# Attention of a two-layer trunk: heads handled in pairs, probabilities times v as 512-column products

## The chip, the cores and the metric

One core of a Trainium2 chip runs the whole kernel as one program. The metric is the device time of one execution in microseconds (us), the median of several runs. The engines are TensorE (PE in the profile, with its weight loads as PEld), VectorE (DVE), ScalarE (ACT), GpSimd (POOL) and SyncE (SP, which issues most DMAs).

## The reference

Two layers are computed on a latent stream (256 tokens) and a context stream (256 tokens), each 2048 wide. Each layer projects the normalized, modulated input into three branches; the one that matters here is attention: 8 query heads of 128, 2 key/value heads (4 query heads share one), rotary positions on the latent tokens, a learned sink in the softmax. Latent queries see 256 context keys and their window of latent keys in one softmax; context queries see context keys only. Context is needed from layer 0 alone, so layer 1 has latent queries only.

```python
s_loc = where(mask, q @ kw * scale, NEG_INF);  s_ctx = q @ k_ctx * scale
p = softmax(concat([sink, s_ctx, s_loc]))
o = p_ctx @ v_ctx + p_loc @ vw                 # latent queries, 256 x 128 per head
p = softmax(concat([sink, q_c @ k_c * scale])) # context queries, layer 0
o_c = p[..., 1:] @ v_c
y = concat([gMLP * silu(g), attention * silu(g), fourier * silu(g)]) @ w_out
```

Everything is float32 in and out.

## The kernel before

**Precision and products.** The kernel computes float32 products from pairs: every operand is split into a high part (`fp32r`, rounded by a copy on ACT, line 507) and a low part (the rest, by a subtraction on DVE, line 508: `split_into`). A product is then three: hi x hi, hi x lo, lo x hi (`mm3`, lines 489 to 492). In layer 1 the latent input holds both halves side by side, so that a step is one product of 512 columns (line 627) and one of 256 (line 629); ACT copies one half of the sum and DVE adds the other (`joined`, lines 609 to 614).

**Units.** The input projection is a chain of units of PE work, one for 128 output columns: `tunit` (layer 0, both streams, 512 columns) and `tunit1` (layer 1). Weights come through the stream `W`: a DMA into a raw tile, a high half on ACT (whi, line 458), a low half on DVE (wlo, line 460). In between, `pace` feeds steps of the modulation, which DVE computes alone (`mod_dve`, lines 250 and 252, and `mod_gate1`, line 290).

**Order.** PE's order is the order of the program text as it is run. Work that needs results of other engines is put off by generators: `later.add(attention(h, ps))` starts one for each head after its q unit, each `yield x` lets x us of units pass (planned time, counted by `later.tick`), and `later.flush` ends all. `YQ`, `YA` and `YB` (line 344) are the pauses of attention in the two layers: from q to scores, from scores to transposes, and between transposes. The order of ACT, DVE and the DMA queues is set by a scheduler from the same program.

**Attention** (lines 944 to 1013), per head: rotate q (`rope`, four copies on ACT, three operations on DVE, then the split into a hi and a lo tile); scores into `ps_sc` (and `ps_scc` for context queries in layer 0); mask and maximum on DVE; exponentials on ACT into probability tiles, two of 128x512 and in layer 0 a third for the context queries; scale by 1/den on ACT (line 985). Then in halves (three in layer 0, two in layer 1): four transposes of 128x128 into `ps_tp` (line 1005), split into a hi and a lo tile of 512 columns, and, one step later, six products of 256 columns with v into `ps_o` (`pv`, by `mm3`). A half is two key blocks of 128 x two query blocks. At the end one copy of o on ACT (line 1013). Gate units (`bg`) follow the eight q units, and multiply o by silu of the gate; `flush` runs before the last of them.

**Rooms.** Temporaries of 128x512 (2 KB per partition) come from one pool of seven tiles, `w2k` (lines 74 and 81): the probabilities, q's halves, the halves of split transposes, and the temporary of `rope`. PSUM has six tiles `mm` (units, scores, o) and two `ms` (transposes). `rots` are four rooms of 128x256 in a tile `mgl`, used by `rope` in turn (line 929). Tiles `yo4` to `yo11` receive the heads' outputs in layer 0 and are empty until then; `hl0` to `hl7` are empty in layer 1 after the projection's context part; `acc`, `rbs` and `join` have other uses earlier or later.

Of the kernel before, what the change touches and what calls it, by code (L numbers as in the profile page):

```python
# [7 lines left out]
F32 = mybir.dt.float32  # L8
F32R = mybir.dt.float32r
BF16 = mybir.dt.bfloat16  # L10
AF = mybir.ActivationFunctionType
ALU = mybir.AluOpType

P = 128
D = 2048
KT = D // P
S = 256
T = 2 * S
EPS = 1e-6
SCALE = 128 ** -0.5  # L20
# [46 lines left out]
def trunk_kernel(ctx: ExitStack, tc: tile.TileContext, xT, xhalf, cT, wss, wsl, wmod, win, wout0, wout1, const, vec, rows,  # L67
                 wmat, bs, sink, out):
    nc = tc.nc
    V, A, G, PE, DMA = nc.vector, nc.scalar, nc.gpsimd, nc.tensor, nc.sync  # L70
# [6 lines left out]
    def sb(shape, dt, tag, bufs=1):  # L77
        cnt[0] += 1
        return pool.tile(shape, dt, tag=tag, bufs=bufs, name=f"{tag}_{cnt[0]}")

    def w2k(shape, dt=F32):
        return sb(shape, dt, "w2k", W2K)

    def mm_ps(name="mm"):
        cnt[0] += 1
        return psum.tile([P, 512], F32, tag="mm", bufs=6, name=f"ps_{name}_{cnt[0]}")

    def ms_ps(name="ms"):
        cnt[0] += 1
        return psum.tile([P, 512], F32, tag="ms", bufs=2, name=f"ps_{name}_{cnt[0]}")  # L90


    yo = [sb([P, T], F32, f"yo{k}") for k in range(KT)]
# [42 lines left out]
    ident = identr.bitcast(F32)  # L136
# [204 lines left out]
    YH = 2.0  # L341
    NX, AHEADX, LATE = 4, 2, 12
    YX, YC, YE = [2.4, 1.4, 1.8], 1.5, 5.0
    YQ, YA, YB = [5.5, 6.8], [10.0, 8.6], [3.8, 4.0]

    def pace():

# [141 lines left out]
    def mm3(ps, st, mv, start, stop):  # L489
        PE.matmul(ps, st[0], mv[0], start=start, stop=False)  # L490
        PE.matmul(ps, st[0], mv[1], start=False, stop=False)  # L491
        PE.matmul(ps, st[1], mv[0], start=False, stop=stop)  # L492

    def part(w, c):

        def of(t):
            if not isinstance(t, list):
                return t[:, c]
            n = t[0].shape[-1]
            return t[c.start // n][:, c.start % n:c.start % n + c.stop - c.start]  # L500

        return of(w[0]), of(w[1])
# [3 lines left out]
    def split_into(hi, lo, src):  # L506
        A.copy(hi, src)  # L507
        V.tensor_tensor(out=lo, in0=src, in1=hi.bitcast(F32), op=ALU.subtract)  # L508
        return hi, lo
# [36 lines left out]
    hl = [None] * KT  # L546
# [42 lines left out]
    FULL, LAT, CTX = slice(0, T), slice(0, S), slice(S, T)  # L589
# [54 lines left out]
    def layer(l):  # L644
        last = l == 1
        n = S if last else T
        nt = n // P
        ysl = (lambda k: y1[k] if k < 4 else yo[k][:, S:T]) if last else (lambda k: yo[k])
        y1 = {}
        if last:  # L650
            a = sb([P, 4, 256], F32, "macc")
            c = [sb([P, 2, S], F32, f"kt{j}") for j in range(2)]
# [166 lines left out]
        if l == 0:  # L819
# [4 lines left out]
            with low(LOWC):  # L824
                for name in ("m0", "ct", "nst"):
                    o, w = COFF[name]
# [97 lines left out]
        def rope(hi, lo, ps, ctx=None):  # L924

            if ctx is None and hi.shape[-1] > S:
                ctx = ps[:, S:T]
            nrot[0] += 1
            rot = rots[nrot[0] % 4]
            for a in range(4):  # L930
                b = a ^ 1
                A.copy(rot[32 * a:32 * a + 32], ps[32 * b:32 * b + 32, 0:S])
            t = w2k([P, S])
            V.tensor_tensor(out=t, in0=ps[:, 0:S], in1=cc("cos"), op=ALU.mult)
            V.tensor_tensor(out=rot, in0=rot, in1=cc("sin"), op=ALU.mult)
            V.tensor_tensor(out=rot, in0=rot, in1=t, op=ALU.add)
            split_into(hi[:, LAT], lo[:, LAT], rot)
            if hi.shape[-1] > S:
                split_into(hi[:, CTX], lo[:, CTX], ctx)

        kt, vv = [], None
        rots, nrot = [], [0]

        def attention(h, ps):
            g = h // 4
            q = w2k([P, n], F32R), w2k([P, n], F32R)
            rope(*q, ps)
            yield YQ[l]
            sc, mx = [], sb([P, 4], F32, "mx", 2)
            for b in range(2):  # L950
                s = mm_ps("sc")
                mm3(s, part(q, slice(b * P, (b + 1) * P)), kt[g], True, True)
                edge = s[:, (1 - b) * P:(2 - b) * P]
                V.tensor_tensor(out=edge, in0=edge, in1=split["m0"][:, b], op=ALU.add)
                sc.append((s, T))
                V.tensor_reduce(out=mx[:, b:b + 1], in_=s, axis=mybir.AxisListType.X, op=ALU.max)
            if not last:
                s = mm_ps("scc")
                for b in range(2):
                    mm3(s[:, b * S:(b + 1) * S], part(q, slice(S + b * P, S + (b + 1) * P)),  # L960
                        part(kt[g], CTX), True, True)
                sc.append((s, S))
                V.tensor_reduce(out=mx[:, 2:4], in_=s.rearrange("p (b k) -> p b k", k=S),
                                axis=mybir.AxisListType.X, op=ALU.max)
            nm = sb([P, 4], F32, "nm", 2)
            V.tensor_scalar(out=nm[:, :nt], in0=mx[:, :nt], scalar1=-SCALE, scalar2=nskb[:, h:h + 1],
                            op0=ALU.mult, op1=ALU.min)
            es = sb([P, 4], F32, "es", 2)
            A.activation(es[:, :nt], nm[:, :nt], AF.Exp, bias=skb[:, h:h + 1])
            den = sb([P, 4], F32, "den", 2)  # L970
            prob = []
            for i, (s, w) in enumerate(sc):
                p = w2k([P, T])
                for b in range(T // w):
                    c = i + b
                    A.activation(p[:, b * w:(b + 1) * w], s[:, b * w:(b + 1) * w], AF.Exp, scale=SCALE,
                                 bias=nm[:, c:c + 1], accum_out=den[:, c:c + 1])
                prob.append(p)
            V.tensor_tensor(out=den[:, :nt], in0=den[:, :nt], in1=es[:, :nt], op=ALU.add)
            V.reciprocal(den[:, :nt], den[:, :nt])  # L980
            for i, (s, w) in enumerate(sc):
                for b in range(T // w):
                    c = i + b
                    with low(LOWP[l]):
                        A.activation(prob[i][:, b * w:(b + 1) * w], prob[i][:, b * w:(b + 1) * w], AF.Copy,  # L985
                                     scale=den[:, c:c + 1])
            yield YA[l]
            o, pts = None, []

            def pv(half):  # L990
                for j in range(2):
                    kk = 2 * half + j
                    dst, kv = (o[:, LAT], kk) if half < 2 else (o[:, CTX], 2 + j)
                    mm3(dst, part(vv, slice(kv * 256 + g * P, kv * 256 + (g + 1) * P)),
                        part(pts[half], slice(j * S, (j + 1) * S)), kk in (0, 4), kk in (3, 5))

            halves = 2 if last else 3
            for half in range(halves):
                tp = ms_ps("tp")
                for j in range(2):  # L1000
                    for b in range(2):
                        kk = 2 * half + j
                        src = prob[b][:, kk * P:(kk + 1) * P] if half < 2 else \
                            prob[2][:, b * S + j * P:b * S + (j + 1) * P]
                        PE.transpose(tp[:, (2 * j + b) * P:(2 * j + b + 1) * P], src, ident)  # L1005
                pts.append(split_into(w2k([P, 512], F32R), w2k([P, 512], F32R), tp))
                if half == 0:
                    o = mm_ps("o")
                else:
                    pv(half - 1)  # L1010
                yield YB[l]
            pv(halves - 1)
            A.copy(ysl(4 + h), o[:, 0:n])

        def gate(k, ps):
            assert not last or k < 4 or k in state["ctx"]
# [29 lines left out]
            later.flush()  # L1046
        r = sb([P, 4, S], F32, "mgl")
        state["phase"] = f"k{l}"
        rots += [r[:, i] for i in range(4)]
        for j in range(2):  # L1050
            pss = tunit1([0, 1]) if last else [tunit(T)]
            kt.append((sb([P, T], F32R, f"kt{j}"), sb([P, T], F32R, ("ws", "bsb")[j])))
# [2 lines left out]
        vv = sb([P, 1024], F32R, "vv"), sb([P, 1024], F32R, "mg")  # L1055
        vps = [mm_ps("v") for _ in range(4)]
        for k in range(KT):
            if k % 4 == 0:
                w = W.next()
# [9 lines left out]
        for h in range(8):  # L1069
            ps = tunit1([0])[0] if last else tunit(n)  # L1070
            later.add(attention(h, ps))
            later.tick(0.0)
# [8 lines left out]
        src = [ysl(k) for k in range(KT)]  # L1081
# [153 lines left out]
    rbs = {}  # L1235
# [90 lines left out]
    with tc.manual_schedule(engines={EN.PE}):  # L1326
# [11 lines left out]
        for k in range(KT):  # L1338
# [7 lines left out]
            c = slice(32 * (k % 4), 32 * (k % 4) + 32)  # L1346
# [28 lines left out]
        make_h(0, 0, rb0, [0, 1], e)  # L1375
        list(e)
        layer(0)
        state["acc"] = out_proj()
        layer(1)
        finish()  # L1380

# [76 lines left out]
```

## Time and profile before

| | before |
|---|---|
| runs (median, lowest to highest) | 1128.75 us (1128.7 to 1129.28), n = 3 |
| the profiled execution: time / span | 1129.38 us / 1127.6 us |
| mean granted clock of PE | 0.999 |
| PE busy, share of span | 1118.0 us, 99% |
| DVE busy | 927.4 us, 82% |
| ACT busy | 526.8 us, 47% |
| DMA, mean | 209 GB/s |

The span is the time from the first to the last instruction of the trace; the profiled execution's time holds 1.8 us more around it. A row of a timeline has start (us), time taken (us), engine, line, operation, output<-input by the program's names, and shape; in square brackets stands the idle time before it and who ended it. Products on PE are pipelined: a row's time is longer than the distance to the next start, and the distance is what PE pays.

### The profile page before, as it was taken

Reading aid. Unit: us, or ns where it says so; the run is one execution under the profiler, and the core shown is the slowest. Engines: PE = TensorE matmul, PEld = TensorE weight load, DVE = VectorE, ACT = ScalarE, POOL = GpSimd, SP = SyncE. Lnnn points to the kernel's source line nnn. Section 1 sums busy time; section 2 is a strip of 40 time slices with the busy share of each in tenths; the row PEclk is TensorE's granted clock in tenths of the full one; section 3 lists DMA queues with packets and bytes.
Section 4 is the critical chain, followed back from the end, with each engine's and each line's share of the span. In section 5 each row is a group of like instructions: output and inputs, shape, how many; then the busy total and the mean of one; then the engine's idle time right before and its main releaser. Section 6 shows DMA issues by size and latency. Waiting matters only on the chain.

```text
span 1127.6 us, 16631 instructions
## 1 busy us (share of the span) xinstructions
PE 1118.0 (99%) x6105; PEld 920.2 (82%) x6108; DVE 927.4 (82%) x1633; ACT 526.8 (47%) x992; POOL 32.8 (3%) x43
## 2 busy tenths in 40 slices
PE   8999999999999999999999999999999999999998
PEld 3666788888888888888888888988888888888886
DVE  1578799989988897888999988396898689968883
ACT  5322433322234667632523334266665369867551
POOL 0000000000000000000000000030500000000000
PEclk9999999999999999999999999999999999999999
DMA  9999656566655343365556665285956786555972
GB/s 360 402 402 400 245 175 202 172 204 193 217 183 187 116 142 130 122 205 172 184 181 215 219 208 185 94 191 200 223 172 199 223 286 206 160 163 187 301 263 75
DMA packets 75138, 235.85 MB, mean 209 GB/s; under 512 B 8608, under 2 KB 13104, under 8 KB 75056
## 3 DMA queue, kind: packets, MB, share of 16 engines
q1 hardware_dynamic: 70272, 229.79, 60.7%
q0 software_dynamic: 4064, 3.69, 2.2%
q10 hardware_dynamic: 720, 1.31, 0.3%
q8 instruction: 48, 0.79, 0.3%
q14 instruction: 34, 0.28, 0.1%
HBM read 232.65 MB, written 2.10 MB: 208 GB/s over the span
## 4 chain that ended last, share of the span: by engine, by line
PE 97%; DVE 1%; DMA 1%; ACT 0%; issue 0%; POOLq 0%; DVEq 0%; POOL 0%; ACTq 0%
PE ps_t L490 15%; PE ps_t L491 15%; PE ps_t L492 15%; PE ps_t L627 10%; PE ps_t L629 5%; PE ps_v L1063 3%; PE ps_y L490 3%; PE ps_y L492 3%; PE ps_y L491 3%; PE ps_mod L182 2%; PE ps_av L490 2%; PE ps_av L491 2%; PE ps_av L492 2%; PE ps_tp L1005 2%; PE ps_v L1065 1%; PE ps_au L490 1%
## 5 line engine op out<-in xcount | busy, mean ns | idle before, releaser
L458 ACT CAST whi<-raw 128x1024 fp32r<-128x1024 f32 (+1 forms) x209 | 216.4, 1037 | 314.1 <-PE ps_t L491 219.4
L460 DVE TENSOR_TENSOR wlo<-raw,whi 128x1024 fp32r<-128x1024 f32 (+1 forms) x209 | 251.0, 1205 | 57.3 <-ACT whi L458 47.1
L490 PE MATMUL ps_t<-hh,whi 128*128 128x512 f32 (+1 forms) x752 | 290.7, 387 | 0.0
L491 PE MATMUL ps_t<-hl,whi 128*128 128x512 f32 (+1 forms) x752 | 289.6, 385 | 0.0
L492 PE MATMUL ps_t<-hh,wlo 128*128 128x512 f32 (+1 forms) x752 | 289.4, 385 | 0.0
L252 DVE SCALAR_TENSOR_TENSOR macc<-mraw,cs,macc 128x512 f32<-128x512 f32 x360 | 251.0, 748 | 11.1 <-DMA mraw<-in_wmod_dram 10.9
L492 PEld LDWEIGHTS ps_t<-hh,wlo 128*128 128x128 f32 x752 | 141.3, 188 | 28.6
L490 PEld LDWEIGHTS ps_t<-hh,whi 128*128 128x128 f32 x752 | 141.3, 188 | 27.0
L491 PEld LDWEIGHTS ps_t<-hl,whi 128*128 128x128 f32 x752 | 141.4, 188 | 26.1
L627 PE MATMUL ps_t<-hh,whi 128*128 128x512 f32 x512 | 139.2, 395 | 0.0
L627 PEld LDWEIGHTS ps_t<-hh,whi 128*128 128x128 f32 x512 | 91.4, 189 | 15.0
L629 PEld LDWEIGHTS ps_t<-hh,wlo 128*128 128x128 f32 x512 | 71.5, 190 | 4.5
L629 PE MATMUL ps_t<-hh,wlo 128*128 128x256 f32 x512 | 74.9, 282 | 0.0
L572 ACT ACTIVATE hh<-w2k,sh 128x256 fp32r<-128x256 f32 x48 | 22.0, 502 | 73.6 <-DVE w2k L568 73.6
L490 PE MATMUL ps_y<-whi,hh 128*128 128x512 f32 x104 | 41.3, 398 | 0.0
L492 PE MATMUL ps_y<-whi,hh 128*128 128x512 f32 x104 | 40.6, 390 | 0.0
L491 PE MATMUL ps_y<-wlo,hh 128*128 128x512 f32 x104 | 40.5, 389 | 0.0
L490 PE MATMUL ps_av<-whi,hh 128*128 128x512 f32 x94 | 39.0, 415 | 0.6 <-ACT hh L572 0.6
L491 PE MATMUL ps_av<-wlo,hh 128*128 128x512 f32 x94 | 37.0, 394 | 0.0
L507 ACT CAST w2k<-ps_tp 128x512 fp32r<-128x512 f32 x40 | 23.3, 582 | 21.1 <-PE ps_scc L491 13.7
L508 DVE TENSOR_TENSOR w2k<-ps_tp,w2k 128x512 fp32r<-128x512 f32 x40 | 27.5, 687 | 3.3 <-ACT w2k L507 2.0
L985 ACT ACTIVATE w2k<-w2k,den 128x512 f32<-128x512 f32 (+1 forms) x48 | 28.1, 645 | 0.4 <-DVE den L980 0.2
(460 smaller groups left out, 1721.9 us busy)
## 6 DMA issues: line engine op xcount, KB each, us to landing
raw<-in_win_dram SPq DMA_DIRECT2D x160, 512.0 KB, 4.1
mraw<-in_wmod_dram SPq DMA_DIRECT2D x128, 512.0 KB, 4.3
raw<-in_wout_dram SPq DMA_DIRECT2D x60, 512.0 KB, 4.3
mraw<-in_wsl_dram SPq DMA_DIRECT2D x14, 512.0 KB, 7.2
yo<-in_wsl_dram SPq DMA_DIRECT2D x16, 256.0 KB, 7.1
macc<-in_wsl_dram SPq DMA_DIRECT2D x7, 512.0 KB, 7.8
vv<-in_wsl_dram SPq DMA_DIRECT2D x7, 512.0 KB, 8.4
mg<-in_wsl_dram SPq DMA_DIRECT2D x7, 512.0 KB, 9.0
```

The costliest lines, as they stand in the source:

```text
L252: V.scalar_tensor_tensor(out=acc[:, s], in0=w[:, kk % 2], scalar=c, in1=acc[:, s], op0=ALU.mult, op1=ALU.add)
L458: A.copy(ph, rc)
L460: self.last = V.tensor_tensor(out=pl, in0=rc, in1=ph.bitcast(F32), op=ALU.subtract)
L490: PE.matmul(ps, st[0], mv[0], start=start, stop=False)
L491: PE.matmul(ps, st[0], mv[1], start=False, stop=False)
L492: PE.matmul(ps, st[1], mv[0], start=False, stop=stop)
L507: A.copy(hi, src)
L508: V.tensor_tensor(out=lo, in0=src, in1=hi.bitcast(F32), op=ALU.subtract)
L627: PE.matmul(ps, wk, h, start=k == 0, stop=False)
L629: PE.matmul(ps[:, 0:S], wk, h[:, 0:S], start=False, stop=k == KT - 1)
L985: A.activation(prob[i][:, b * w:(b + 1) * w], prob[i][:, b * w:(b + 1) * w], AF.Copy, scale=den[:, c:c + 1])
L1063: PE.matmul(vps[t], hs[t][0], wk, start=k == 0, stop=False)
```

## The change

Heads are taken in pairs (0 and 1, 2 and 3, ...). The even head ends after its softmax and parks its probabilities; after the odd head's softmax a new generator, `pair_pv`, does transposes and products of both: each step kk takes one key block of 128 for both heads (two heads x two query blocks = four transposes), splits the 512 columns, and one step later multiplies them with v in three products of 512 columns, low half first. Layer 0 has six steps a pair (four for latent, two for context queries), layer 1 four. o of a pair is one PSUM tile of 512 columns for latent queries and one for context queries; ACT copies it in two pieces of 256.

Rooms (`room`): in layer 1 all probabilities lie in `hl0` to `hl7`, two per head, the first four heads' rooms being used again by the last four. In layer 0 an odd head keeps three `w2k` tiles; heads 0 and 2 lie in `yo4` to `yo9`, heads 4 and 6 in `yo10`, `acc`, two `rbs`, and `yo11`, the upper half of `mgl` and two `join`. For that `rope` uses two rooms of `mgl` in layer 0 instead of four. `YB` of layer 0 goes from 3.8 to 3.4.

```diff
-    YQ, YA, YB = [5.5, 6.8], [10.0, 8.6], [3.8, 4.0]
+    YQ, YA, YB = [5.5, 6.8], [10.0, 8.6], [3.4, 4.0]
...
+        paired = {}
+        def room(h):
+            def thirds(t):
+                return [t[:, 0:S], t[:, S:T]]
+            if last:
+                return [sb([P, T], F32, f"hl{h % 4 * 2 + i}") for i in range(2)]
+            if h % 2:
+                ts = [w2k([P, T]) for _ in range(3)]
+            elif h < 4:
+                ts = yo[4 + 3 * h // 2:7 + 3 * h // 2]
+            else:
+                ts = [yo[8 + h // 2], sb([P, T], F32, "acc") if h == 4 else spare]
+                return ts + [[sb([P, S], F32, "rbs" if h == 4 else "join", 2) for _ in range(2)]]
+            return ts[:2] + [thirds(ts[2])]
+
+        def pair_pv(g, h):
+            o, pts = {}, []
+            def pv(kk):
+                kv, dst = (kk, o[0]) if kk < 4 else (kk - 2, o[1])
+                st, (hi, lo) = part(vv, slice(kv * 256 + g * P, kv * 256 + (g + 1) * P)), pts[kk]
+                for a, b in ((st[0], lo), (st[0], hi), (st[1], hi)):
+                    PE.matmul(dst, a, b, start=kk in (0, 4) and b is lo, stop=kk in (3, 5) and a is st[1])
+                if kk in (3, 5):
+                    for i in range(2):
+                        A.copy(ysl(4 + h - 1 + i)[:, slice(kk // 5 * S, kk // 5 * S + S)], dst[:, i * S:(i + 1) * S])
+            for kk in range(4 if last else 6):
+                tp = ms_ps("tp")
+                for i in range(2):
+                    for b in range(2):
+                        pr = paired[h - 1 + i]
+                        src = pr[b][:, kk * P:(kk + 1) * P] if kk < 4 else pr[2][b][:, (kk - 4) * P:(kk - 3) * P]
+                        PE.transpose(tp[:, (2 * i + b) * P:(2 * i + b + 1) * P], src, ident)
+                pts.append(split_into(w2k([P, 512], F32R), w2k([P, 512], F32R), tp))
+                if kk % 4 == 0:
+                    o[kk // 4] = mm_ps("o")
+                if kk:
+                    pv(kk - 1)
+                yield YB[l]
+            pv(len(pts) - 1)
...
-            prob = []
+            paired[h] = prob = room(h)
...
-            yield YA[l]
-            o, pts = None, []
-            def pv(half):
-                for j in range(2):
-                    kk = 2 * half + j
-                    dst, kv = (o[:, LAT], kk) if half < 2 else (o[:, CTX], 2 + j)
-                    mm3(dst, part(vv, slice(kv * 256 + g * P, kv * 256 + (g + 1) * P)),
-                        part(pts[half], slice(j * S, (j + 1) * S)), kk in (0, 4), kk in (3, 5))
-            halves = 2 if last else 3
-            for half in range(halves):
...
-                yield YB[l]
-            pv(halves - 1)
-            A.copy(ysl(4 + h), o[:, 0:n])
+            if h % 2:
+                yield YA[l]
+                yield from pair_pv(g, h)
...
-        rots += [r[:, i] for i in range(4)]
+        rots += [r[:, i] for i in (range(4) if last else (0, 1, 0, 1))]
+        spare = r[:, 2:4].rearrange("p a b -> p (a b)")
```

More of the change, by code (lines that the diff above doesn't have):

```diff
@@ L970, in attention @@
             den = sb([P, 4], F32, "den", 2)
-            prob = []
+            paired[h] = prob = room(h)
             for i, (s, w) in enumerate(sc):
-                p = w2k([P, T])
                 for b in range(T // w):
[L975 to L978, printed above, removed]
+                    A.activation(prob[i][b] if i == 2 else prob[i], s[:, b * w:(b + 1) * w], AF.Exp, scale=SCALE,
+                                 bias=nm[:, i + b:i + b + 1], accum_out=den[:, i + b:i + b + 1])
             V.tensor_tensor(out=den[:, :nt], in0=den[:, :nt], in1=es[:, :nt], op=ALU.add)
@@ L982, in attention @@
                 for b in range(T // w):
-                    c = i + b
+                    p = prob[i][b] if i == 2 else prob[i]
                     with low(LOWP[l]):
-                        A.activation(prob[i][:, b * w:(b + 1) * w], prob[i][:, b * w:(b + 1) * w], AF.Copy,
-                                     scale=den[:, c:c + 1])
-            yield YA[l]
-            o, pts = None, []
-            def pv(half):
-                for j in range(2):
-                    kk = 2 * half + j
-                    dst, kv = (o[:, LAT], kk) if half < 2 else (o[:, CTX], 2 + j)
-                    mm3(dst, part(vv, slice(kv * 256 + g * P, kv * 256 + (g + 1) * P)),
-                        part(pts[half], slice(j * S, (j + 1) * S)), kk in (0, 4), kk in (3, 5))
-            halves = 2 if last else 3
-            for half in range(halves):
[L999 to L1010, printed above, removed]
-                yield YB[l]
-            pv(halves - 1)
-            A.copy(ysl(4 + h), o[:, 0:n])
+                        A.activation(p, p, AF.Copy, scale=den[:, i + b:i + b + 1])
+            if h % 2:
+                yield YA[l]
+                yield from pair_pv(g, h)
         def gate(k, ps):
```

## The prediction

> **What bounds the kernel now.** I read the first page from the top, then the waits of TensorE (PE), then the tiles that the change touches, then the timeline at single places. On the page: busy time of each engine, the granted clock, and the chain of work that ended last.
>
> ```profile
> span 1127.6 us, 16631 instructions
> ...
> PE 1118.0 (99%) x6105; PEld 920.2 (82%) x6108; DVE 927.4 (82%) x1633; ACT 526.8 (47%) x992; POOL 32.8 (3%) x43
> ...
> PEclk9999999999999999999999999999999999999999
> ...
> PE 97%; DVE 1%; DMA 1%; ACT 0%; issue 0%; POOLq 0%; DVEq 0%; POOL 0%; ACTq 0%
> ```
>
> PE is busy 99% of the span at full clock, and 97% of the chain that ended last is PE. So time changes in two ways only: PE's own work becomes shorter or longer, or PE waits where it did not. The waits of PE, over the whole run (total us, times, longest):
>
> ```profile
> PE ps_idle L535 <- DVE red L112: 2.0, 1, 2.0
> PE ps_sc L492 <- DVE w2k L508: 0.7, 1, 0.7
> ...
> PE ps_f L490 <- DVE w2k L873: 0.2, 1, 0.2
> ```
>
> The first belongs to the start of the kernel. In attention (about 355 to 510 us in layer 0, 910 to 1010 in layer 1) there is one, a score product (ps_sc) that waited 0.7 us for the low half of a q. No product of probabilities and v waits at all.
>
> **The change, part by part.** *Work of PE.* The view of the tiles gives the products that are replaced and the transposes that feed them (min/median/max ns):
>
> ```profile
> L490 PE MATMUL ps_o<-w2k,vv x80: 279/282/367, 376.9 to 1007.1; 128*128 128x256 f32 x80
> L491 PE MATMUL ps_o<-w2k,vv x80: 277/279/388, 377.1 to 1007.2; 128*128 128x256 f32 x80
> L492 PE MATMUL ps_o<-w2k,mg x80: 276/279/283, 377.2 to 1007.3; 128*128 128x256 f32 x80
> L1013 ACT COPY yo<-ps_o x16: 366/481/588, 391.0 to 1007.6; 128x512 f32<-128x512 f32 x8, 128x256 f32<-128x256 f32 x8
> ```
> ```profile
> L1005 PE MATMUL ps_tp<-identr,w2k x160: 270/272/273, 369.9 to 1001.4; 128*128 128x128 f32 x160
> L507 ACT CAST w2k<-ps_tp x40: 560/585/595, 370.6 to 1001.8; 128x512 fp32r<-128x512 f32 x40
> L508 DVE TENSOR_TENSOR w2k<-ps_tp,w2k x40: 669/691/692, 371.9 to 1002.4; 128x512 fp32r<-128x512 f32 x40
> ```
>
> 240 products of 256 columns become 120 of 512 (72 in layer 0, 48 in layer 1, counted in the order of the changed kernel). The 160 transposes, in 40 groups, and their 40 splits keep number and shape. Durations overlap, since products are pipelined; what PE pays is the distance of starts:
>
> ```profile
> 375.66 0.39 PE L492 MATMUL ps_t<-hh,wlo 128*128 128x512 f32 x1
> ...
> 376.57 0.60 PE L1005 MATMUL ps_tp<-identr,w2k 128*128 128x128 f32 x4
> 376.93 0.36 PE L490 MATMUL ps_o<-w2k,vv 128*128 128x256 f32 x1
> 377.13 0.28 PE L491 MATMUL ps_o<-w2k,vv 128*128 128x256 f32 x1
> ...
> 377.71 0.39 PE L490 MATMUL ps_t<-hh,whi 128*128 128x512 f32 x1
> ```
>
> From 375.66 stand four 512-column products before 376.57: 0.91/4 = 0.2275 us each. From 377.13 stand five of 256 columns before 377.71: 0.58/5 = 0.116. The first product behind transposes takes 0.20, so 0.08 more; there are 40 groups of transposes before and after, so this surcharge stays. Gain: 120 x (2 x 0.116 - 0.2275) = 120 x 0.0045 = **-0.5 us**. The starts are read to 0.01 us; bounds are 0.001 and 0.011 per product, -0.1 and -1.3 us. The Trainium skill ("TensorE: Matmul & The Clock Gate", section "Back-to-back issue gap") gives the distance of warm products as columns/2.4 + 2.5 ns, which speaks against the change: a product of half the length costs only 2.5 ns more per pair. By that the sum would be -0.3 us; the trace has both lengths some 7 to 12 ns slower than it, with 4.5 ns per pair.
>
> *Work of the other engines.* Exponentials, scales and splits keep their number. Layer 0 copies o in 16 pieces of 256 columns instead of 8 of 512: by the copy's row (366 the shortest, 588 the longest) 16 x 0.37 - 8 x 0.59 = 1.2 us of ScalarE (ACT) over 150 us. ACT is 47% busy; I cost it at nothing by itself, and count it in the chain below. The smaller YB (3.4 for 3.8) only places groups.
>
> *Parking and later transposes.* A pair's transposes start only when the odd head has its probabilities, some 13 us later in layer 0 and 6 in layer 1. The last product of a pair still comes before the gate units end, so nothing is late for the gates. But the odd heads of layer 0 hold three of the seven w2k tiles from their softmax until the last transposes of the pair, and while those run, head h+2's probabilities, head h+3's q (hi and lo) and the split transposes want tiles too. In the order of the changed kernel, followed by its semaphores, this bites at two places, both of layer 0: pair 0 (under head 4's unit of q) and pair 1 (under head 6's). There the low half of the split of transposes 4 (w2k, L508 on VectorE, DVE) goes into the tile that held context probabilities which transposes 5 read last. Transposes 5 stand on PE directly before the first product of step 4, and that product takes this low half first. So PE must finish the transposes, let DVE split, and only then go on: no other work lies between. Elsewhere the split is over 5 us ahead of its product.
>
> The price, with the rows of one such turn from PE over ACT to DVE:
>
> ```profile
> 490.59 0.60 PE L1005 MATMUL ps_tp<-identr,w2k 128*128 128x128 f32 x4
> 490.95 0.36 PE L490 MATMUL ps_o<-w2k,vv 128*128 128x256 f32 x1
> ```
> ```profile
> 491.23 0.59 ACT L507 CAST w2k<-ps_tp 128x512 fp32r<-128x512 f32 x1 [2.60 <-PE ps_tp L1005]
> ```
> ```profile
> 919.97 0.42 DVE L508 TENSOR_TENSOR w2k<-mgl,w2k 128x256 fp32r<-128x256 f32 x1
> ```
> ```profile
> 920.45 0.50 PE L492 MATMUL ps_sc<-kt,w2k 128*128 128x512 f32 x1 [0.75 <-DVE w2k L508]
> 920.79 0.39 PE L490 MATMUL ps_sc<-kt,w2k 128*128 128x512 f32 x1
> ```
>
> Transposes end 0.60 after their first start, where the next product would start at 0.36; the next engine starts 0.04 later (491.19 to 491.23); the split is 0.69; DVE's end to PE's start is 0.06 (920.39 to 920.45). Restart of the product: 0.60 + 0.04 + 0.69 + 0.06 - 0.36 = **1.0 us** if DVE is free. The product after that idle takes 0.34 to the next start (920.45 to 920.79) instead of 0.23, but this one had its surcharge of 0.08 already. That is pair 1: by the order, ACT and DVE have done q's splits a microsecond before. I take 1.05, bounds 1.0 and 1.5.
>
> In pair 0 DVE is not free. Ahead of the split in its queue stand, after the rotation of q: a weight's low half, q's two low halves, and three steps of the modulation (L252). DVE works in order, as does ACT. The rows of the same chain behind an earlier q unit:
>
> ```profile
> 364.50 1.49 ACT L932 COPY mgl<-ps_t 32x256 f32<-32x256 f32 x4
> 366.02 1.05 ACT L458 CAST whi<-raw 128x1024 fp32r<-128x1024 f32 x1
> 367.09 0.37 ACT L507 CAST w2k<-ps_t 128x256 fp32r<-128x256 f32 x1
> 367.36 0.73 ACT L985 ACTIVATE w2k<-w2k,den 128x512 f32<-128x512 f32 x1
> 367.99 0.40 ACT L507 CAST w2k<-mgl 128x256 fp32r<-128x256 f32 x1
> ```
> ```profile
> 366.03 0.42 DVE L934 TENSOR_TENSOR w2k<-ps_t,cst 128x256 f32<-128x256 f32 x1 [1.14 <-ACT mgl L932]
> ...
> 368.42 0.43 DVE L508 TENSOR_TENSOR w2k<-mgl,w2k 128x256 fp32r<-128x256 f32 x1
> 368.76 0.42 DVE L508 TENSOR_TENSOR w2k<-ps_t,w2k 128x256 fp32r<-128x256 f32 x1
> ...
> 375.49 2.07 DVE L252 SCALAR_TENSOR_TENSOR macc<-mraw,cs,macc 128x512 f32<-128x512 f32 x3
> ```
>
> Count from the start of the last product of head 4's unit. ACT: product ends 0.39, rots 0.43 to 1.92, whi to 2.97, q's context half to 3.3, then (new) two copies of o at 0.3 to 0.37 to 3.95, a scale to 4.6, q's latent half to 5.0. DVE: its low half then at 5.03, the second to 5.8, three L252 (2.07) to 7.85, the split (0.69) to 8.55, PE at 8.6. PE would be there after 25 products of 0.2275 (5.69), one group of transposes with surcharge (0.36 + 0.09) and the second group (0.36): 6.5. So 2.1 us; with ACT's and DVE's instructions closing up by 0.2 to 0.4 as their starts do above, 1.7. I take **1.9 us**, bounds 1.05 (the steps of L252 have no time to stand in the way) and 2.8 (one more step of 0.67 or its data late).
>
> Sum for layer 0: 1.9 + 1.05 = +2.95. Pairs 2 and 3 lie under gate units, which need no q, and tiles suffice.
>
> *Layer 1.* Eight hl tiles hold the probabilities, w2k is free of them, and no such turn is in the order. Both engines are nearly full there, though (busy PE, PEld, DVE, ACT of the stretch):
>
> ```profile
> 930.00:950.00 20.00, 20.00 (x122) 17.40 (x121) 18.86 (x40) 18.77 (x39) 0.00 (x0) 1.00 0.62 201
> ```
> ```profile
> 933.88 0.42 DVE L508 TENSOR_TENSOR w2k<-mgl,w2k 128x256 fp32r<-128x256 f32 x1
> ```
> ```profile
> 934.94 0.40 PE L492 MATMUL ps_sc<-kt,w2k 128*128 128x512 f32 x1
> ```
>
> Here q's low half ended 0.64 us before its score product (934.30 to 934.94). Without transposes between them the scores of heads 1 to 3 follow at about 7.0 us (16 x 0.23 + 16 x 0.12 of the unit, 6 x 0.23 of scores) instead of up to 9.3 with two groups, so this margin shrinks; by the order I find 0.2 to 0.3 left at head 3 and between 0 and -0.8 at head 4. I take 0, bounds 0 and +1.1. The wait of 0.7 at 920 lies before the order changes and stays; were it to go, -0.9 (with the slow restart).
>
> Forecast: -0.5 + 2.95 + 0 = +2.45. The profiled execution took 1129.38, its span of 1127.6 and 1.8 around it, so it would be 1131.8; the median of the runs, 1128.75, is 0.6 less: **1131.2 us**. The clock should not move: the row of the stretch above, and the PEclk line, show it full through all of attention, the wait of 0.75 at 920 included.
>
> **The rivals.** *Gain alone* (the side that is not slower): the two turns are hidden, which needs the low halves to land in tiles free earlier than I read the semaphores. For it: before has no such wait. Against: the product follows the transposes directly. It gives 1128.75 - 0.5 = 1128.2 (1127.4 to 1128.9).
> *ACT and DVE fall behind in layer 1*: scores at 7.0 us, engines 94% busy. From the point where the margin of 0.64 is used up, each of heads 2 to 5 pays what the wait at 920 cost, 0.75 + 0.11: up to 4 x 0.86 = 3.4 on top, 1132.5 to 1134.6. Against: before the transposes start ACT has less to do (no splits).
> *Faster by more than 2.3*: the surcharge of 0.08 vanishes with long products (40 x 0.08 = 3.2), or the wait at 920 goes and the gain is at its bound. A 512-column score product behind transposes speaks against it:
>
> ```profile
> 370.28 0.48 PE L490 MATMUL ps_sc<-kt,w2k 128*128 128x512 f32 x1
> 370.60 0.39 PE L491 MATMUL ps_sc<-ws,w2k 128*128 128x512 f32 x1
> ```
>
> It took 0.32, still 0.09 more. With the surcharge gone and no new wait: 1125.0.
> That the change does not do what it says I rule out: its order holds the 120 products.
>
> **How the numbers follow.** Forecast with its own bounds (1129.5 to 1132.9): 0.58. Gain alone: 0.18. Layer 1 behind: 0.17. Faster: 0.07. What this kernel's measurement can tell from no change is about 0.2%, 2.26 us, so same is 1126.5 to 1131.0. The forecast lies just above that edge; I give 0.25 of its 0.58 to below. Same: 0.25 + 0.18 = 0.43; slower: 0.33 + 0.17 = 0.50; faster 0.07. The range leaves out the faster case and the upper half of the layer 1 case, and cuts the gain alone at its middle: 1128.1 to 1133.3.
>
> **What would show it.** In the waits of PE: two entries of ps_o for a low half of DVE, one near 1.9 and one near 1.05 us, near 415 and 448 us, and none of ps_o in layer 1. In the tiles: 120 products of ps_o, 0.2275 apart. Clock 1.00. Wrong would be: no ps_o wait in layer 0, waits of ps_sc for L508 between 930 and 970 of over 1 us, or the turn in pair 0 at 1.0 (then L252 does not stand in the way).

## The result, and the profile after

The changed kernel took 1133.13 us (median of 7, 1132.19 to 1133.81), the kernel before 1129.09 us in the same session: ratio 1.0034, 95% interval 1.0024 to 1.0043, so slower by 3.8 us (2.7 to 4.9). The forecast was +2.45, and 1133.13 us lies near the upper end of the stated range (1128.1 to 1133.3). The profiled execution of the changed kernel took 1133.81 us, its span is 4.4 us longer than before's. In its lines 970 is a product with v, 981 a transpose, 973 the copy of o, 1028 the scale of probabilities, and 1020 the exponential.

```profile
span 1132.0 us, 16369 instructions
...
PE 1119.1 (99%) x5985; PEld 914.9 (81%) x5988; DVE 927.3 (82%) x1633; ACT 525.8 (46%) x1000; POOL 32.9 (3%) x43
...
PEclk9999999999999999999999999999999999999999
```

PE issues 120 products less and is still busy 99% of a longer span, at full clock. The share of busy time does not show what was lost, so the waits have to be read for themselves. Waits of PE in the changed kernel (total us, times, longest):

```profile
PE ps_o L970 <- DVE w2k L508: 2.0, 2, 1.1
PE ps_idle L535 <- DVE red L112: 2.0, 1, 2.0
PE ps_sc L492 <- DVE w2k L508: 1.5, 2, 0.9
PE ps_av L491 <- DVE wlo L460: 0.8, 1, 0.8
```

Two waits of ps_o are new, as forecast; ps_sc waits twice instead of once; a weight's low half is late at the start of layer 1. Where the 4.4 us come from is read by landmarks, products that both kernels have, as first and last start in the views of tiles. Before, then after:

```profile
L272 PE MATMUL ps_modc<-red,cst x24: 224/229/235, 379.9 to 700.3; 128*32 128x32 f32 x24
...
L492 PE MATMUL ps_av<-whi,hh x32: 389/391/397, 738.7 to 770.7; 128*128 128x512 f32 x32
...
L1065 PE MATMUL ps_v<-wlo,hl x48: 278/280/283, 321.2 to 905.9; 128*128 128x256 f32 x48
...
L490 PE MATMUL ps_y<-whi,hh x104: 389/389/481, 1026.5 to 1107.8; 128*128 128x512 f32 x104
```
```profile
L272 PE MATMUL ps_modc<-red,cst x24: 224/229/235, 378.2 to 703.1; 128*32 128x32 f32 x24
...
L492 PE MATMUL ps_av<-whi,hh x32: 387/389/397, 741.5 to 774.7; 128*128 128x512 f32 x32
...
L1084 PE MATMUL ps_v<-wlo,hl x48: 278/280/283, 321.1 to 909.5; 128*128 128x256 f32 x48
...
L490 PE MATMUL ps_y<-whi,hh x104: 389/389/481, 1031.0 to 1112.3; 128*128 128x512 f32 x104
```

Layer 0's attention lost 2.8 us (738.7 to 741.5). The start of layer 1 lost another 1.2 up to the last ps_av (770.7 to 774.7), from one wait:

```profile
771.57 0.50 PE L491 MATMUL ps_av<-wlo,hh 128*128 128x512 f32 x1 [0.76 <-DVE wlo L460]
```

Of that 0.8 is left at the last ps_v (905.9 to 909.5), since the kernel before waits near 800 for a w2k tile of line 873 (ps_f, 0.2 in its waits, 0.3 by starts) and the changed kernel does not. Layer 1's attention lost 0.9 more (1026.5 to 1031.0 against 905.9 to 909.5), with two score products (ps_sc) that wait for the low half of a q:

```profile
924.52 0.50 PE L492 MATMUL ps_sc<-kt,w2k 128*128 128x512 f32 x1 [0.89 <-DVE w2k L508]
954.89 0.50 PE L492 MATMUL ps_sc<-kt,w2k 128*128 128x512 f32 x1 [0.61 <-DVE w2k L508]
```

A turn here is a wait of PE for another engine that itself had to wait for PE. The turn of pair 0 in the changed kernel, on PE and then on DVE (steps and their transposes are counted from 0):

```profile
413.51 0.38 PE L981 MATMUL ps_tp<-identr,yo 128*128 128x128 f32 x2
413.72 0.38 PE L981 MATMUL ps_tp<-identr,w2k 128*128 128x128 f32 x2
415.23 0.74 PE L970 MATMUL ps_o<-w2k,vv 128*128 128x512 f32 x2 [1.13 <-DVE w2k L508]
```
```profile
412.18 0.42 DVE L508 TENSOR_TENSOR w2k<-ps_t,w2k 128x256 fp32r<-128x256 f32 x1
412.51 2.07 DVE L252 SCALAR_TENSOR_TENSOR macc<-mraw,cs,macc 128x512 f32<-128x512 f32 x3
414.49 0.68 DVE L508 TENSOR_TENSOR w2k<-ps_tp,w2k 128x512 fp32r<-128x512 f32 x1
```

Transposes 5 end at 414.10; the split that had to wait for them starts at 414.49, since three steps of L252 are ahead of it until then; PE goes on at 415.23. Without the wait the product would start 0.36 after the first transpose, at 413.87: 1.36 us lost. The turn of pair 1 (DVE, then PE):

```profile
448.68 0.69 DVE L508 TENSOR_TENSOR w2k<-ps_tp,w2k 128x512 fp32r<-128x512 f32 x1 [1.21 <-PE ps_tp L981]
```
```profile
447.97 0.38 PE L981 MATMUL ps_tp<-identr,yo 128*128 128x128 f32 x2
448.19 0.38 PE L981 MATMUL ps_tp<-identr,w2k 128*128 128x128 f32 x2
449.42 0.73 PE L970 MATMUL ps_o<-w2k,vv 128*128 128x512 f32 x2 [0.85 <-DVE w2k L508]
```

DVE was free here: 449.42 - 447.97 - 0.36 = 1.09 us. Three more steps of layer 0 are late by less than the view of waits shows, because a row of PE lasts longer than the distance to the next start, so that PE still counts as busy. They are found as distances of starts: 408.08 to 408.60 for the last two transposes (0.14 otherwise), 0.38 lost, and 0.10 and 0.16 near 443 and 477.

### The profile page after: what moved, and what is told of

Same layout as the page of the kernel before. It is cut to its first block, busy times and chain, and to the rows that moved or that the text cites. A ratio compares the mean times of both kernels' runs of the same rounds, so it can differ in the third digit from the quotient of the medians.

```text
span 1132.0 us, 16369 instructions
## 1 busy us (share of the span) xinstructions
PE 1119.1 (99%) x5985; PEld 914.9 (81%) x5988; DVE 927.3 (82%) x1633; ACT 525.8 (46%) x1000; POOL 32.9 (3%) x43
## 4 chain that ended last, share of the span: by engine, by line
PE 89%; DMA 4%; DVE 3%; ACT 2%; issue 1%; POOL 0%; ACTq 0%; POOLq 0%; DVEq 0%; SPq 0%
PE ps_t L490 15%; PE ps_t L491 15%; PE ps_t L492 15%; PE ps_t L627 9%; PE ps_t L629 5%; PE ps_v L1082 3%; PE ps_y L490 3%; PE ps_y L492 3%; PE ps_y L491 3%; PE ps_o L970 2%; PE ps_mod L182 2%; PE ps_av L490 2%; PE ps_tp L981 1%; PE ps_av L491 1%; PE ps_v L1084 1%; PE ps_av L492 1%
## 5 line engine op out<-in xcount | busy, mean ns | idle before, releaser
L252 DVE SCALAR_TENSOR_TENSOR macc<-mraw,cs,macc 128x512 f32<-128x512 f32 x360 | 250.0, 745 | 8.2 <-DMA mraw<-in_wmod_dram 7.7
L970 PE MATMUL ps_o<-w2k,vv 128*128 128x512 f32 x80 | 27.8, 429 | 2.1 <-DVE w2k L508 2.0
```

The costliest lines, as they stand in the source:

```text
L252: V.scalar_tensor_tensor(out=acc[:, s], in0=w[:, kk % 2], scalar=c, in1=acc[:, s], op0=ALU.mult, op1=ALU.add)
L970: PE.matmul(dst, a, b, start=kk in (0, 4) and b is lo, stop=kk in (3, 5) and a is st[1])
```

## The experiments

Each ran beside the kernel before, and ratios are to it; 1.0009 is about 1 us. A delay "by starts" is a distance of starts less the usual one.

**room**: a tile more, without more memory.

```diff
-                ts = [w2k([P, T]) for _ in range(3)]
+                ts = [w2k([P, T]), w2k([P, T]), yo[10 + h // 2] if h < 4 else w2k([P, T])]
```

> The changed kernel, with the third probability tile of heads 1 and 3 in yo10 and yo11 (empty until heads 4 and 6 need them) instead of w2k. Theory: the two long waits of ps_o in layer 0 (1.37 and 1.10 us beyond the usual distance of starts) come from the tile that transposes 5 still read; with more tiles free both are gone, the time is 2.5 us below the changed kernel, about 1.3 us above the kernel before (ratio 1.001). Rival: DVE's queue is late at these places whatever tile it writes; then the waits keep at least half, and the time is within 1 us of the changed kernel (ratio 1.003).

Measured: 1130.01 us, ratio 1.0011 (1.0002 to 1.0019). Its waits of PE have no ps_o left:

```profile
PE ps_idle L535 <- DVE red L112: 2.0, 1, 2.0
PE ps_sc L492 <- DVE w2k L508: 1.5, 2, 0.9
PE ps_rs L1366 <- ACT w2k L1359: 0.6, 1, 0.6
```

The two turns are the tile's doing, and the time is as the theory has it. By starts, delays of 0.38, 0.24 and 0.13 stay at three steps.

**hifirst**: order of the three products of a step.

```diff
-                for a, b in ((st[0], lo), (st[0], hi), (st[1], hi)):
+                for a, b in ((st[0], hi), (st[1], hi), (st[0], lo)):
```

(start and stop follow the new first and last product.)

> The changed kernel, with the three products of a step in the order hi, hi, low half instead of low half first. Theory: DVE's low half is what PE waits for in all five late steps of layer 0 (0.38, 1.37, 0.10, 1.10, 0.16 us); two products of 0.23 now stand ahead of it, so each wait loses up to 0.46: to 0, 0.91, 0, 0.64, 0, in sum 1.56 us below the changed kernel, about 2.2 above before (ratio 1.002). Rival: ACT's high half is late too, or the wait only moves behind the first two products: no change, ratio 1.0034.

Measured: 1131.09 us, ratio 1.0015 (1.0006 to 1.0024). The waits that are left:

```profile
PE ps_o L970 <- DVE w2k L508: 1.0, 2, 0.6
```

From the third product's start back to the second's the turns are 1.02 and 0.78 us instead of 0.23: 0.79 and 0.55 lost, where it was 1.36 and 1.09. Each wait shrank by 0.54 to 0.57, a little more than the cover of 0.46; of the small ones, the first is 0.22 instead of 0.38 and the others are gone. The theory holds for the waits (1.56 left of 3.09). By the landmark at 738.7 layer 0 gains less, 1.2 us: behind each of the three late products the next one starts 0.34 later, not 0.23.

**only0** and **only1**: pairs in one layer, the other as before (the code of before behind `if not last` or `if last`, with its rooms and YB).

```diff
+            if not last:      # only0; "if last" in only1
+                if h % 2:
+                    yield YA[l]
+                    yield from pair_pv(g, h)
+                return
+            yield YA[l]
...
```

> Pairs in layer 0 alone; layer 1 handles heads singly as before, with products of 256 columns. Theory: the waits of layer 0 stay and layer 1's attention is as before: +2.7 us (ratio 1.0024), with ps_sc waiting once, near 924. The wait of 0.8 us for a weight in the start of layer 1 (ps_av for wlo) is a late DMA of that execution and is not in it. Rival: that wait follows from the changed layer 0: it is there again and the time is +3.5 (ratio 1.003).

> Pairs in layer 1 alone; layer 0 handles heads singly as before. Theory: no wait of ps_o in layer 0, and in layer 1 the low half of head 4's q is late (0.77 us and slow restart near 951), against a gain of about 0.4 in products: +0.5 to +0.9 us (ratio 1.0004 to 1.0008). Rival (layer 1 costs nothing, the late q came of the shifted layer 0): within 0.3 us of before or below it.

Measured: only0 1131.94 us, ratio 1.0021 (1.0013 to 1.0030); only1 1129.76 us, ratio 1.0005 (0.9996 to 1.0014). Layer 0 has most of the loss. Layer 1's part is not clear of noise, since the interval of only1 holds 1; the sum 2.4 + 0.6 = 3.0 agrees with 3.8 within the intervals. only1 has no wait of ps_o in layer 0, and its ps_sc waits twice, near 919 and 950, as in the changed kernel; so the second is layer 1's own. only0 has the wait of ps_av for wlo, against the theory there (see **again**).

**room_hi**: both edits of layer 0.

> Both edits together: the third tile of heads 1 and 3 in yo10 and yo11, and high halves first. Without the tile edit the low half came late in five steps of layer 0, with it in three (0.38, 0.24, 0.13 us over the usual distance); two products of 0.23 ahead cover each of these. Theory: no wait of ps_o is left in layer 0, 0.75 us below the kernel with the tile edit alone: about +0.5 us against before (ratio 1.0005). Rival: the three small delays are not the low half's, and the ratio stays at 1.0011.

Measured: 1129.87 us, ratio 1.0008 (0.9999 to 1.0017). One delay of 0.19 stays, at 408; the landmark at 738.7 is at 738.5. Layer 0 is then level with before; what is left lies in layer 1. The ratio lies between the theory's 1.0005 and the rival's 1.0011, and its interval holds both; the starts, with two of the three delays gone, speak for the theory.

**room_hi_yq** and **before_yq**: a longer pause from q to scores in layer 1.

```diff
-    YQ, YA, YB = [5.5, 6.8], [10.0, 8.6], [3.4, 4.0]
+    YQ, YA, YB = [5.5, 8.0], [10.0, 8.6], [3.4, 4.0]      # room_hi_yq; before_yq: [5.5, 8.0], [10.0, 7.4], [3.8, 4.0]
```

> The same, and in layer 1 the scores 1.2 us of units later (YQ 6.8 to 8.0). Theory: what layer 1 loses is q's low half, late at the scores near 919 (1.05 us) and 950 (0.77 us); with 1.2 us more both waits go, and the gain of the long products is seen: 1.9 us below the kernel without this edit, -1.3 us against before (ratio 0.9988). Rival: ACT and DVE, 93 to 99% busy there, only pass the delay on to later heads: within 0.5 us of the kernel without the edit.

> The kernel before, heads singly, with scores of layer 1 later by the same 1.2 us and the transposes where they were (YQ 8.0, YA 7.4). Theory: its one wait of attention, near 920 (0.91 us over the usual distance), goes: -0.9 us (ratio 0.9992), and what is left between this kernel and the one with pairs and the same pause is the gain of the products, 0.4 to 0.8. Rival: the wait moves to another head; within 0.3 us of before.

Measured: 1135.03 us, ratio 1.0051 (1.0038 to 1.0063), and 1150.39 us, ratio 1.0189 (1.0175 to 1.0203). Both theories fell. The waits of ps_sc did go, but others came. room_hi_yq, waits of PE, then ACT:

```profile
PE ps_o L970 <- ACT w2k L507: 4.0, 3, 1.7
```
```profile
944.57 1.65 ACT L932 COPY mgl<-join 32x256 f32<-32x256 f32 x4
946.25 1.34 ACT L1028 ACTIVATE hl<-hl,den 128x512 f32<-128x512 f32 x2
947.49 0.39 ACT L507 CAST w2k<-mgl 128x256 fp32r<-128x256 f32 x1
947.79 0.36 ACT L612 COPY join<-ps_t 128x256 f32<-128x256 f32 x1
948.05 0.58 ACT L507 CAST w2k<-ps_tp 128x512 fp32r<-128x512 f32 x1
```

The transposes of that split started at 940.64; ACT, without a pause since 935, came to it at 948.05, 7 us later. The rival has the mechanism right (ACT passes the delay on) but not the size: it said within 0.5 us of room_hi, and it is 5.2. In before_yq the probabilities still lie in w2k, q stays in it longer, and PE waits at nearly every head:

```profile
PE ps_o L490 <- ACT w2k L507: 7.8, 5, 3.0
PE ps_o L491 <- DVE w2k L508: 6.7, 10, 1.5
```

Its distances of 1.457 and 0.726 between a group's transposes, first and second product repeat at four heads, the pattern of a turn: transposes end, ACT splits, PE, DVE splits, PE. Whether tiles or ACT set each of these was not taken apart. Part of this loss is the clock: behind the wait of 3.0 us that ends at 940.9, the granted clock of PE is 0.5 from about 941.1 to 944.5, and again from 982.1 to 985.5. Products of 256 columns start 0.21 apart there instead of 0.12. A row of stretches (start and end, then busy time of PE, PEld, DVE, ACT and POOL, granted clock, DMA share, GB/s):

```profile
942.00:943.00 1.00, 1.00 (x6) 1.00 (x6) 0.00 (x0) 0.09 (x2) 0.00 (x0) 0.50 0.83 320
```

By these numbers 1.7 us of work are lost each time, an estimate. What brought the clock down the second time, behind waits of 1.5 us and less, is open.

**room_hi_rate** and **before_rate**: modulation steps out of the q units of layer 1.

```diff
-                k1=2.5, v1=2.5, q1=1, bg1=0.3, out1=1.4)
+                k1=2.5, v1=2.5, q1=0, bg1=1.3, out1=1.4)
```

> Pairs with both edits of layer 0 (tile and high half first), and in layer 1 the modulation steps of DVE (L290, two of 0.75 us and one DMA each) moved from the eight q units to the eight gate units (rates q1 0, bg1 1.3 instead of 1 and 0.3). YQ is as in the changed kernel. Theory: the scores of layer 1 wait because DVE, with these steps in its queue, is late with q's low half (1.05 us near 919, 0.79 near 950 over the usual distance); without them both waits go and no turn of tiles comes in their place: 1.8 us below the kernel without this edit, -1.0 us against before (ratio 0.9991), the first one below it. Rival: ACT is the late one (99% busy from 930 to 950), DVE only follows: the wait at 950 stays, ratio 1.0000 to 1.0008.

> The kernel before with the same move of L290 from q to gate units in layer 1. Theory: its wait near 920 (0.91 us over the usual distance) goes, nothing else changes: -0.9 us (ratio 0.9992); the pairs' own gain is then what the kernel with pairs and this edit is below this one: 0.1 to 0.8. Rival: the wait stays, since it is the DMA of the raw weights that is late: within 0.3 us of before.

Measured: 1129.98 us, ratio 1.0008 (1.0000 to 1.0017), and 1129.94 us, ratio 1.0008 (0.9999 to 1.0017). The wait at 950 went, which fits a part of L290 in it, though ACT's order changed as well. But in both kernels the scores near 918 now wait for ACT, and a smaller wait stands near 934. room_hi_rate:

```profile
PE ps_sc L490 <- ACT w2k L507: 1.2, 1, 1.2
...
PE ps_sc L492 <- DVE w2k L508: 0.4, 1, 0.4
```

The scheduler orders ACT and DVE anew, and the first q's rotation comes later. Neither theory nor rival as stated: the wait changed its place and engine. The two kernels are 0.04 us apart, so the gain of 0.1 to 0.8 that was expected of the pairs is not seen.

**rhq76**: scores 0.8 later, transposes where they were (YQ 7.6, YA 7.8 of layer 1, with both edits of layer 0).

> Pairs with both edits of layer 0, and in layer 1 scores 0.8 us later with the pause after them 0.8 shorter (YQ 7.6, YA 7.8), so that the transposes stand where they stood and only the scores move. Theory: the long pause of 8.0 failed since it pushed transposes into a stretch where ACT already ran 7 us behind; with the transposes in place the waits for q's low half (1.04 and 0.79 us over the usual distance) shrink to 0.25 and 0: 1.5 us below the kernel with the two edits alone, -0.7 us against before (ratio 0.9994). Rival: ACT, which has no free time from 930 to 950, is the limit, and whatever pause is chosen one product waits for it: ratio 1.0008 or more.

Measured: 1129.85 us, ratio 1.0003 (0.9994 to 1.0012). No score stands in the list of waits (one is 0.24 late by starts, near 951), and one group of transposes now waits for its PSUM tile, whose last content DVE has yet to split:

```profile
PE ps_tp L981 <- DVE w2k L508: 1.3, 1, 1.3
```

The ratio lies between the theory's 0.9994 and the rival's 1.0008, and its interval holds both; something on PE waits here too, though for DVE and not, as in the rival, for ACT. It is the lowest ratio with pairs in both layers, but not told apart from room_hi; no version here beats the kernel before.

**halves2**: short products in the changed order.

```diff
-                    PE.matmul(dst, a, b, start=kk in (0, 4) and b is lo, stop=kk in (3, 5) and a is st[1])
+                    for i in range(2):
+                        PE.matmul(dst[:, i * S:(i + 1) * S], a, b[:, i * S:(i + 1) * S], start=kk in (0, 4) and b is lo and i == 0,
+                                  stop=kk in (3, 5) and a is st[1] and i == 1)
```

> The changed kernel with each product of 512 columns issued as two of 256 over the two heads, half after half: 240 products as before; pairs, rooms and order as in the changed kernel. Theory: a pair of short products takes 0.232 to 0.236 us from start to start, a long one 0.231, so the products of ps_o take 0.1 to 0.6 us more than in the changed kernel, in all; the waits of ps_o in layer 0 stay (1.4 and 1.1). Rival: short products hide their weight load less well in this order: over 1 us more.

Measured: 1133.47 us, ratio 1.0036 (1.0023 to 1.0048). Summed from each ps_o start to the next start on PE, the 240 short products take 30.92 us, the changed kernel's 120 long ones 30.59: 0.33 us, 2.8 ns per pair. The long ones vary by some 0.06 from profile to profile (30.53 in room). For the products the theory holds, in its lower half. Of the waits it does not: by starts three products of ps_o are late, 1.14, 1.10 and 1.09, the first of them at the place near 408 where the changed kernel lost 0.38. The Trainium skill ("TensorE: Matmul & The Clock Gate", section "Back-to-back issue gap") gives a warm product 2.5 ns beside the time of its columns; for 120 products that is 0.3 us, an estimate. The trace agrees with this difference.

**again**: the changed kernel once more.

> The changed kernel unaltered, for a second profile of it. Theory: the waits of ps_o in layer 0 (1.37 and 1.10) and of ps_sc in layer 1 (about 1.05 and 0.77) come again within 0.2, and the wait of ps_av for wlo near 770 (0.8) comes only if the weights' DMA takes over 6.3 us from issue to its split; time 1.0030 to 1.0034 of before. Rival: that wait belongs to the change and comes again with a DMA as quick as that of the kernel before (5.1 us).

Measured: 1132.44 us, ratio 1.0029 (1.0019 to 1.0039). Waits of PE:

```profile
PE ps_o L970 <- DVE w2k L508: 2.2, 2, 1.3
...
PE ps_sc L492 <- DVE w2k L508: 0.6, 1, 0.6
...
PE ps_av L491 <- DVE wlo L460: 0.6, 1, 0.6
```

The turns came again, 1.58 and 1.10 us by starts, the first 0.2 longer. The score near 952 again lost 0.77; the one near 922 lost 0.31 instead of 1.06, with the weight's raw tile there earlier: ACT waits 1.13 us for it in the changed kernel, 0.73 in before, and not at all in again. The wait of ps_av belongs to a DMA of layer 1's Fourier weights, seen from issue (SP queue) to the split that waits for it (ACT). Before, after:

```profile
759.35 0.42 SPq L839 DMA_DIRECT2D w2k<-in_wmat_dram  x1
```
```profile
764.43 0.62 ACT L507 CAST vv<-w2k 128x512 fp32r<-128x512 f32 x1 [2.57 <-DMA w2k<-in_wmat_dram]
```
```profile
762.08 0.43 SPq L839 DMA_DIRECT2D w2k<-in_wmat_dram  x1
```
```profile
768.68 0.62 ACT L507 CAST vv<-w2k 128x512 fp32r<-128x512 f32 x1 [4.09 <-DMA w2k<-in_wmat_dram]
```

5.1 against 6.6 us. In the other profiles: 6.9 in again and rhq76, 7.1 in room_hi_yq, 6.3 in only0, all with the wait; 4.4 to 6.3 in the remaining eight, without it. The wait goes with a late DMA, with 6.3 us on both sides (only0 has it, room_hi not), and the rival falls. Open is whether pairs in layer 0 make the DMA late: with layer 0 as before it took 4.9 to 5.2 in four profiles, with pairs 4.4 to 7.1 in ten.

## Why the prediction was right or wrong, point by point

- **PE bound; only new waits can cost.** Right: the granted clock was full, and the landmarks move by the waits.
- **Product gain -0.5.** Right in sign and small; halves2 measures 0.33. 0.01 us of reading was too coarse for 4.5 ns.
- **Two turns, at pair 0 and pair 1, none in pairs 2 and 3.** Right in place and cause (room). Pair 1: 1.05 forecast, 1.09 measured.
- **Turn of pair 0: 1.9.** Measured 1.36. The split started when the count said (L252 until about 414.5), but PE came later than counted, 0.38 having been lost one step before. Together 1.74.
- **"Elsewhere the split is over 5 us ahead of its product."** Wrong, for three steps (0.38, 0.10, 0.16). The distance from transposes to product was 5 us, but not that from the split. All three are step 3 of their pair (0, 1 and 2), and ACT came to its high half only behind exponentials, 3.4 to 3.7 us after the transposes had ended (406.64, 441.69, 475.85). In pair 0 DVE was later still, at 407.88, behind modulation steps, one of which had waited for its DMA. Layer 0 in sum: 2.95 forecast, 3.09 measured in waits, 2.8 net. That the sum fits is in part luck: pair 0's turn was 0.54 smaller than forecast, and the three delays, forecast at nothing, make 0.64.

```profile
406.64 0.60 ACT L507 CAST w2k<-ps_tp 128x512 fp32r<-128x512 f32 x1
```
```profile
407.88 0.66 DVE L508 TENSOR_TENSOR w2k<-ps_tp,w2k 128x512 fp32r<-128x512 f32 x1
```

- **Layer 1: 0, bounds 0 and +1.1.** This is the mis-sized term: +0.9 net in this profile. Head 4's q was late by 0.77, at the end of the bounds that the order gave (0 to -0.8), and I took the other end. The scores near 920, put down as unchanged, make 0.5 more than in before; their wait varies from 0.3 to 1.06 with the DMA of raw weights. Against these stand the shorter products (0.13) and 0.4 that before loses to late low halves at two products of ps_o near 946 and 948, too short for its list of waits. So the 0.9 is not the change's alone: from the last ps_v to the first ps_y it is 120.6 us in before, 121.5 in the changed kernel, 120.4 in again and 120.0 in only0, and the last two, both with 0.31 near 922, differ by 0.4.
- **Start of layer 1.** Not seen: +0.8 in this execution: +1.2 from a late DMA, less 0.4 further on, most of it the wait that before has near 800.
- **Rival "ACT and DVE fall behind".** Not at the four heads it named in the changed kernel, but the mechanism is there: in the stretch that is 930 to 950 in before, and 3.6 us later in the changed kernel, ACT's busy time rose from 18.77 to 19.39 of 20 us (only1, not shifted by layer 0: 19.40), and a longer pause (room_hi_yq) set it 7 us behind.

```profile
933.60:953.60 20.00, 20.00 (x112) 17.29 (x111) 18.04 (x41) 19.39 (x41) 0.00 (x0) 1.00 0.61 201
```

Not tried: the turn of pair 0 with L252 taken out of DVE's queue, and a free choice of the tiles in layer 1. What sets the last 0.3 to 0.9 us of layer 1 is not settled: each edit there moved the wait to another place.

## What to carry to other kernels

Joining short products into long ones saved only a fixed cost of each here, 0.3 us of 1129 with PE busy 99% of the span, and it is worth looking first at what the joining holds on to. Ask of every tile that lives longer which write takes its room next, and whether the engine that frees it is the one that waits for that write: a turn of that kind costs the whole way over the other engine, about 1.1 us here, whatever distance the plan shows. Order operands so that the one ready last is used last; two products ahead of the low half hid half a microsecond of each wait.

## What was not expected of the hardware

The surcharge of 0.08 to 0.09 us on the first product behind transposes is the same for 256 and 512 columns, whether that product is a score, one of a unit or one with v. The DMA of one 256 KB tile issued at the same place of the program took 4.4 to 7.1 us to its first use over 14 profiles, enough to decide a wait of 0.8 us on PE. In before_yq, with PE waiting for up to 3.0 us, the granted clock fell to 0.5 for 3.4 us twice; in attention of the kernel before and of the changed kernel, with no wait over 0.7 and 1.1 us, it stayed at 1.00.
